# Splitting weight units ahead of their use, and storing transposed activations in pieces

## The chip, the cores and the metric

The kernel runs on one core of a Trainium2 chip. Its parts that matter here are TensorE (PE in the profile, with its weight loads as PEld), VectorE (DVE), ScalarE (ACT), GpSimd (POOL), and SyncE (SP), whose queue issues nearly all DMA transfers. The metric is the device time of one execution in microseconds, and the median of several runs is given.

## The reference, cut to what matters

An encoder layer is applied to two sequences of 1024 ("short") and 2048 ("long") tokens, each with 16 meta tokens in front; all weights are shared.

```python
xn = _rmsnorm(h, g_pre)
proj = xn @ w_in + b_in                      # 1024 -> 6672 columns
na_q, na_k, na_v, na_z, ml_qk, ml_v, ml_z, ml_o, ml_g, mg = split(proj)
ya = neighbourhood_attention(na_q, na_k, na_v, na_rpb)
ya = (ya * silu(na_z)) @ w_a
yb = (mlstm_branch(ml_qk, ml_v, ml_g, ml_o, ...) * silu(ml_z)) @ w_b
ga, gb = split(sigmoid(mg))                  # the gates: 2 x 1024 columns
y = (ga * ya + gb * yb) @ w_out              # the merge
return h + _rmsnorm(y, g_post)
```

All of it is in float32. The kernel makes each large product out of three products of a rounded high part and a low remainder: `hi*hi + hi*lo + lo*hi`. So every weight and every activation that enters a product is split first: ACT copies the high part, rounded to the type that PE takes, and DVE (for the first three units POOL) subtracts it from the original to get the low part.

## The kernel before, in words

The work is two streams of Python generators whose instructions are put into one program. The **dense** stream makes the projections and merges, the **sparse** stream the mLSTM and the neighbourhood attention. `run` takes steps of the two in turn by estimated costs; this fixes PE's order, which is written out by hand (`manual_schedule` for PE). The other engines' queues, SP's included, are ordered by the compiler's planner, which takes instructions in the order in which they become ready in its own model, the earlier written first.

The dense stream follows `PLAN`. A group `(s, t0, cols)` projects 1024 tokens of sequence `s` from token `t0` onto the columns of the mLSTM ("m"), the attention ("n") or the gates ("g"); `("f", s, b)` is a merge block of 512 tokens. The order is m and n of the short sequence, m of the long one's first half, m and n of its second half, g of the short sequence, its two merge blocks, and then the rest of the long sequence. The sparse stream follows `STEPS`: short mLSTM, short attention, long mLSTM, long attention.

*Weights.* A weight unit is 512 KB (some are 528): 128 columns of `w_in` by 1024 rows, or 256 columns by 512 rows, or the like of `w_a`, `w_b` and `w_out`. At its first use `wload` (L217) loads it into `wraw` (two buffers), `wpump` splits it (L235 on ACT, L238 on DVE) into `whi` and `wlo` (four buffers each) and stores both to DRAM (L242). At each later use `wpump` loads the stored halves back (L233). There are 68 units. 16 of them belong to the gates, 8 to `w_a` and `w_b`, 8 to `w_out`; these 32 are first used in the short sequence's gate group and its first merge block, beside the long mLSTM.

*Activations.* `build_half` normalises and transposes 512 tokens and splits them into `xh` and `xl` (two buffers each). Where a group of the same tokens comes much later in `PLAN`, it stores the two (L319), each with one transfer of 2 MB; the later group loads them back (L267). This is so for all six halves.

*A merge block* (`final`) multiplies the branch outputs, split by `yload` into `yh` and `yl` (L1217, L1218), with `w_a` and `w_b`, applies the gates `tg` (loaded at L1259, used at L1279 and L1281), splits the result into `mh` and `mlo` (L1282, L1283) and multiplies it with `w_out` (L1300 to L1302).

*The mLSTM* (`ml`) works on blocks of 256 tokens for four heads in turn: `raw`, `va` and `um` are its loads, `kf`, `num`, `den` and `hb` steps of its chain. `ml_norm` normalises 512 tokens of a head on DVE (`hb`, L1184 to L1197), and PE transposes them (L1202) at its place in the written order. The attention (`na`) prepares each head's `stk`, `kd` and `kx` on ACT and DVE (L638 to L645).

*Memory.* The sparse stream's pools lie on the right side of SBUF as a stack, the dense stream's long-lived pool `wp` on the left.

Of the kernel before, what the change touches and what calls it, by code (L numbers as in the profile page):

```python
# [9 lines left out]
F32 = mybir.dt.float32  # L10
F32R = mybir.dt.float32r
I32 = mybir.dt.int32
AF = mybir.ActivationFunctionType
ALU = mybir.AluOpType
# [3 lines left out]
P = 128  # L18
TCARGS = dict(schedule_with_timeline_sim=True)
D = 1024  # L20
KT = D // P
# [3 lines left out]
SEQLEN = (TP, TS)  # L25
# [5 lines left out]
C_MQ, C_MK, C_MV, C_MZ, C_MO, C_GA, C_GB = 2048, 2560, 3072, 3584, 4096, 4624, 5648  # L31
# [10 lines left out]
STEPS = (("ml", 0, ()), ("na", 0, (0, 1)), ("ml", 1, ()), ("na", 1, (0, 1, 2, 3)))  # L42
# [6 lines left out]
def _row_types(R):  # L49

    out = []
    for t in range(R // 8):
        if t == 0:
            out.append((0, 0, 11))
        elif t == R // 8 - 1:
            out.append((2, R - 12, 12))
        else:
            out.append((1, 8 * t - 4, 15))
    return out
# [51 lines left out]
class K:  # L111
# [3 lines left out]
    def __init__(self, tc, ins, outs):  # L115
        self.tc, self.nc = tc, tc.nc
        self.xs = []
        self.nu = 1
        self.i, self.o = ins, outs
        self.wreq, self.wraw, self.wrdy, self.wout = deque(), deque(), deque(), 0  # L120
        self.wseen, self.wkept, self.xkept = set(), {}, {}
        self.side = []


    def rsqrt8(self, pool, v, shape):
# [131 lines left out]
    def build_half(self, s, t0, meta, res, tags=("pj",), xp=None, per=4):  # L257

        nc, wp = self.nc, self.wp
        if (s, t0) in self.xkept:  # L260
            yield
            yield "scaled"
            x = []
            for name, part in zip(("xh", "xl"), self.xkept[s, t0]):
                x.append(wp.tile([P, KT, HALF], F32R, name=name, bufs=2))
                for k in range(0, KT, 4):
                    nc.sync.dma_start(x[-1][:, k:k + 4, :512].bitcast(F32), part[:, k:k + 4, :])  # L267
                yield
            res.append(tuple(x))
            return  # L270
        src = self.i["x_prompt" if s == 0 else "x_sample"]
        base = NM if meta else 0
        jobs = [(src[t0 + P * j:t0 + P * (j + 1), :], P, base + P * j) for j in range(4)]
        js = [jobs[a:a + per] for a in range(0, 4, per)]
        if meta:
            js[-1] = js[-1] + [(self.i["meta"], NM, 0)]
        xh = xl = None
        cnt = 0
        scaled = []
        for grp in js:  # L280
            xs = []
            for ap, n, col in grp:
                xr = (xp or wp).tile([P, D], F32, name="xr", bufs=5 if xp else 4)
                nc.sync.dma_start(xr[:n], ap)
                xs.append((xr, n, col))
            yield
            m = len(grp)
            ss = wp.tile([P, 5], F32, name="ss", bufs=2)
            nc.gpsimd.memset(ss, 1.0)
            for q, (xr, n, _) in enumerate(xs):  # L290
                junk = wp.tile([P, D], mybir.dt.bfloat16, name="xsq", tag="thT", bufs=1)
                nc.scalar.activation(junk[:n], xr[:n], AF.Square, accum_out=ss[:n, q:q + 1])
                yield
            nc.vector.tensor_scalar(ss[:, :m], ss[:, :m], 1.0 / D, EPS, op0=ALU.mult, op1=ALU.add)
            r = self.rsqrt8(wp, ss[:, :m], [P, m])
            yield
            for q, (xr, n, col) in enumerate(xs):
                nc.vector.scalar_tensor_tensor(xr[:n], xr[:n], r[:n, q:q + 1], self.gpre[:n], op0=ALU.mult, op1=ALU.mult)
                yield
            yield "scaled"  # L300
            if xh is None:
                xh = wp.tile([P, KT, HALF], F32R, name="xh", bufs=2)
                xl = wp.tile([P, KT, HALF], F32R, name="xl", bufs=2)
            for xr, n, col in xs:
                for e in range(2):
                    pt = self.psum(tags[cnt % len(tags)], [P, 4, P])
                    cnt += 1
                    for j in range(4):
                        nc.tensor.transpose(pt[:, j, :n], xr[:n, (4 * e + j) * P:(4 * e + j + 1) * P], self.ident[:n, :n])
                    h = xh[:, 4 * e:4 * e + 4, col:col + n]  # L310
                    nc.scalar.activation(h, pt[:, :, :n], AF.Copy)
                    nc.vector.tensor_tensor(xl[:, 4 * e:4 * e + 4, col:col + n], pt[:, :, :n], h.bitcast(F32), op=ALU.subtract)  # L312
                    yield
        where = [j for j, g in enumerate(PLAN) if g[:2] == (s, t0 // 1024 * 1024)]
        if where[-1] - where[0] >= len(where):
            self.xkept[s, t0] = []
            for x, part in ((xh, "h"), (xl, "l")):
                d = self.dp.tile([P, KT, 512], F32, name=f"x{part}{s}_{t0}")
                nc.sync.dma_start(d[:, :, :], x[:, :, base:base + 512].bitcast(F32))  # L319
                self.xkept[s, t0].append(d)  # L320
        res.append((xh, xl))


    def fm_evac(self, col, s, t0, meta, chunks, ps):
# [182 lines left out]
    def group(self, s, t0, meta, cols, reuse, nxt):  # L507

        todo = [(s, t0, meta), (s, t0 + 512, False)]
        jobs = self.layout(cols)  # L510
        nb = None
        for j, (kind, c) in enumerate(jobs):
            if kind == "tm":
                yield from self.tm_unit(c[0], [(x,) + h for x, h in zip(self.xs, todo)], c[1])
                continue
            ws = self.wtake(len(c))
            last = j == len(jobs) - 1
            for hf in range(2):
                side = None
                if j == 0 and hf == 0 and not reuse:  # L520
                    side = self.spread(self.build_half(*todo[1], self.xs), 15)
                elif last and nxt and nxt[0] == "f":
                    side = self.spread(self.ystart(*nxt[1:]), 15) if hf else None
                elif last and nxt:
                    if hf == 0:
                        nres = []
                        nb = self.build_half(*nxt, nres)
                        side = self.spread(nb, 15, "scaled")
                    else:
                        side = self.spread(nb, 15)  # L530
                for col, w in zip(c, ws):
                    for cost in self.fm_half(col, w, self.xs[hf], *todo[hf], done=self.wdone if hf else None):
                        yield cost
                        if side:
                            side()
                        if self.fout:
                            next(self.fout, None)
                if side:
                    side(True)
        if nb:  # L540
            self.xs = nres
# [870 lines left out]

    def sparse(self):

        for kind, s, rts in STEPS:
            if kind == "ml":
                for t0 in range(0, SEQLEN[s], 1024):
                    yield ("m", s, t0)
                yield from self.ml(s)
            else:  # L1420
                types = _row_types(SEQLEN[s] // 64)
                for t0 in range(0, SEQLEN[s], 1024):
                    if any((types[b][1] + types[b][2]) * 64 > t0 for b in rts):
                        yield ("n", s, t0)
                yield from self.na(s, rts)

    def run(self, ctx):
        self.done = set()
        self.setup(ctx)
        dense, acc = self.dense(ctx), 0.0  # L1430
        for w in self.sparse():
            if isinstance(w, tuple):
                while w not in self.done:
                    assert next(dense) is not True
                continue
            acc += w
            while acc > 0.0:
                d = next(dense, None)
                if d is None or d is True:
                    acc = 0.0  # L1440
                    break
                acc -= d
        for w in dense:
            assert w is not True
# [43 lines left out]
```

## Time and profile before

| what | value |
|---|---|
| median of 3 runs | 2904.53 us (2902.79 to 2905.13) |
| profiled execution, its own time | 2912.43 us |
| its span | 2910.7 us |
| PE, DVE, ACT busy | 2820.4, 1749.4, 1293.7 us |
| transferred | 661.88 MB, mean 227 GB/s |
| mean granted clock of PE | 0.989 |

Times in the profile are microseconds from the span's start. "A <- B" in a wait means that the engine of A stood idle until B released it. In a group, "busy, mean ns" are its total and the mean of one instruction; SPq rows are issues of transfers by SP. PEclk is the clock that PE was granted, as a share of full speed.

### The profile page before, as it was taken

How to read it: one execution, taken by the hardware profiler on the slowest of the kernel's cores; microseconds unless marked ns; L12 is line 12 of the kernel's file. 1: busy time of each engine (PE TensorE's matmuls, PEld its weight loads, DVE VectorE, ACT ScalarE, POOL GpSimd, SP SyncE). 2: the span in 40 equal slices, each digit the busy share in tenths (PEclk: the TensorE clock that was granted, in tenths of full speed). 3: DMA queues.
4: the chain of work that ended last, by engine and by line, in shares of the span. 5: the costliest groups of instructions: out<-in, count | busy, mean ns of one | idle time of the engine just before them, and what ended most of it. 6: DMA issues, size and time to landing. Idle time of an engine off the chain costs nothing.

```text
span 2910.7 us, 49314 instructions
## 1 busy us (share of the span) xinstructions
PE 2820.4 (97%) x17488; PEld 2513.6 (86%) x17488; DVE 1749.4 (60%) x4813; ACT 1293.7 (44%) x3114; POOL 23.4 (1%) x107
## 2 busy tenths in 40 slices
PE   6999999999999999999998999999999999999998
PEld 6998898899789988888886988898888888889887
DVE  5232576666556755467669778463555557777843
ACT  4112555444343444355655545453444445545421
POOL 1000000000000000000000000000000000000000
PEclk9999999999999999999999999999999999999999
DMA  9655576754775553578779798546659659888975
GB/s 349 221 178 180 198 230 235 269 185 161 246 233 171 186 170 123 173 249 273 233 249 316 265 341 293 176 140 196 200 180 293 207 166 262 259 289 253 304 255 193
DMA packets 436888, 661.88 MB, mean 227 GB/s; under 512 B 51136, under 2 KB 257296, under 8 KB 436640
## 3 DMA queue, kind: packets, MB, share of 16 engines
q1 hardware_dynamic: 435520, 656.03, 68.9%
q0 software_dynamic: 1120, 2.69, 0.4%
q8 instruction: 138, 2.26, 0.3%
q14 instruction: 110, 0.90, 0.1%
HBM read 447.97 MB, written 210.61 MB: 226 GB/s over the span
## 4 chain that ended last, share of the span: by engine, by line
PE 83%; DMA 9%; DVE 5%; ACT 1%; issue 1%; SPq 0%; DVEq 0%; ACTq 0%
PE pj L144 14%; PE pj L145 14%; PE pj L146 14%; PE pj L409 6%; PE pj L410 6%; PE pj L411 6%; PE sm L700 3%; PE pj L1302 3%; PE pj L1300 3%; PE pj L1301 3%; PE tr L688 3%; PE sc L663 1%; PE sc L664 1%; DMA tg<-gt 1%; PE sm L146 1%
## 5 line engine op out<-in xcount | busy, mean ns | idle before, releaser
L144 PE MATMUL pj<-xh,whi 128*128 128x512 f32 (+1 forms) x1824 | 717.1, 393 | 0.2 <-DVE xl L312 0.2
L145 PE MATMUL pj<-xl,whi 128*128 128x512 f32 (+1 forms) x1824 | 700.3, 384 | 0.4 <-DVE xl L312 0.4
L146 PE MATMUL pj<-xh,wlo 128*128 128x512 f32 (+1 forms) x1824 | 698.5, 383 | 0.0
L409 PE MATMUL pj<-whi,xh 128*128 128x256 f32 (+3 forms) x1576 | 451.8, 287 | 0.0
L410 PE MATMUL pj<-wlo,xh 128*128 128x256 f32 (+3 forms) x1576 | 445.7, 283 | 0.0
L411 PE MATMUL pj<-whi,xl 128*128 128x256 f32 (+3 forms) x1576 | 445.4, 283 | 0.0
L146 PEld LDWEIGHTS pj<-xh,wlo 128*128 128x128 f32 x1824 | 343.9, 189 | 72.1
L144 PEld LDWEIGHTS pj<-xh,whi 128*128 128x128 f32 x1824 | 344.3, 189 | 57.7 <-DVE xl L312 0.8
L145 PEld LDWEIGHTS pj<-xl,whi 128*128 128x128 f32 x1824 | 344.7, 189 | 55.6 <-DVE xl L312 0.7
L409 PEld LDWEIGHTS pj<-whi,xh 128*128 128x128 f32 (+1 forms) x1576 | 295.5, 188 | 1.5 <-issue 0.2
L410 PEld LDWEIGHTS pj<-wlo,xh 128*128 128x128 f32 (+1 forms) x1576 | 295.2, 187 | 1.1
L411 PEld LDWEIGHTS pj<-whi,xl 128*128 128x128 f32 (+1 forms) x1576 | 295.1, 187 | 0.9
L1300 PE MATMUL pj<-whi,mh 128*128 128x256 f32 x768 | 221.7, 289 | 0.0
L671 ACT ACTIVATE prb<-sc,mx 128x384 f32<-128x384 f32 (+2 forms) x192 | 120.1, 625 | 228.1 <-DVE mx L667 221.3
L1302 PE MATMUL pj<-whi,mlo 128*128 128x256 f32 x768 | 218.8, 285 | 1.9 <-DVE mlo L1283 1.9
L1301 PE MATMUL pj<-wlo,mh 128*128 128x256 f32 x768 | 218.4, 284 | 0.0
L691 DVE TENSOR_TENSOR pts<-tr,pts 96x512 fp32r<-96x512 f32 (+2 forms) x192 | 131.9, 687 | 119.2 <-ACT pts L690 117.5
L418 DVE TENSOR_TENSOR stT<-pj,bb 128x256 f32<-128x256 f32 (+3 forms) x197 | 83.3, 423 | 153.7 <-PE pj L411 150.4
L690 ACT ACTIVATE pts<-tr 96x512 fp32r<-96x512 f32 (+2 forms) x192 | 114.0, 594 | 115.9 <-PE tr L688 115.6
L667 DVE CUSTOM_DVE_ANT_1 sc<-sc,gt 128x384 f32<-128x384 f32 (+2 forms) x192 | 118.7, 618 | 76.1 <-PE sc L664 68.3
L144 PE MATMUL pj<-yh,whi 128*128 128x512 f32 x384 | 157.0, 409 | 7.4 <-DVE tg L1279 7.3
L706 DVE TENSOR_TENSOR yg<-sm,yg 64x128 f32<-64x128 f32 x384 | 108.3, 282 | 77.7 <-ACT yg L704 70.1
(233 smaller groups left out, 5123.7 us busy)
## 6 DMA issues: line engine op xcount, KB each, us to landing
whi<-wh SPq DMA_DIRECT2D x176, 512.0 KB
wlo<-wl SPq DMA_DIRECT2D x176, 512.0 KB
wh<-whi SPq DMA_DIRECT2D x64, 512.0 KB
wl<-wlo SPq DMA_DIRECT2D x64, 512.0 KB
wraw<-w_in SPq DMA_DIRECT2D x48, 512.0 KB
gt<-st SPq DMA_DIRECT2D x96, 256.0 KB
tg<-gt SPq DMA_DIRECT2D x96, 256.0 KB
xh<-xh SPq DMA_DIRECT2D x6, 2048.0 KB
```

Of the source, the lines that this page charges most:

```text
L144: mm(out, ah, bh, start=start, stop=False)
L145: mm(out, ah, bl, start=False, stop=False)
L146: mm(out, al, bh, start=False, stop=stop)
L409: nc.tensor.matmul(o, xh, wh, start=k == 0, stop=False)
L410: nc.tensor.matmul(o, xh, wl, start=False, stop=False)
L411: nc.tensor.matmul(o, xl, wh, start=False, stop=k == KT - 1)
L667: nc.vector.tensor_tensor_reduce(out=so, in0=so, in1=gt[:, g0:g0 + ns, c0:c0 + 32], op0=ALU.add, op1=ALU.min, scale=-1.0, scalar=3.0e38, a ...
L671: nc.scalar.activation(pr_[:, :N].rearrange("p (b a c) -> p b a c", b=4, c=8), sc[:, :N].rearrange("p (a b c) -> p b a c", b=4, c=8), AF.E ...
L691: nc.vector.tensor_tensor(pts[:ks, :, 1, :], pt[:ks], pts[:ks, :, 0, :].bitcast(F32), op=ALU.subtract)
L1300: nc.tensor.matmul(o, mh[:, k, xs], wh, start=k == 0, stop=False)
L1301: nc.tensor.matmul(o, mh[:, k, xs], wl, start=False, stop=False)
L1302: nc.tensor.matmul(o, ml[:, k, xs], wh, start=False, stop=k == KT - 1)
```

## The change

There are two parts. First, a generator `wprepare` goes through the 32 units of the gates, `w_a`, `w_b` and `w_out`: it loads a unit into a buffer of its own (`lw`), splits it (the high part into `hw`, the low part in place), and stores both halves to DRAM as `wpump` would have done. Its pool `wx` is opened ahead of the short mLSTM and closed behind it. In the dense stream `beside` is called behind every step of a group; from its 25th call on, every fourth call takes one of the three steps of a unit (load; split; store). What is left when the short mLSTM ends is done at once. When the gate group and the first merge block then ask for these units, `wpump` finds them stored and loads the halves.

Second, `build_half` no longer stores `xh` and `xl` itself but puts 16 pieces of 256 KB a half on a list, and every second call of `beside` issues one.

`sparse` is cut in two functions to hold the pool; the order of PE's work stays.

```diff
@@ __init__
-        self.side = []
+        self.xput, self.turn, self.wlater = deque(), 0, None
@@ build_half
             for x, part in ((xh, "h"), (xl, "l")):
                 d = self.dp.tile([P, KT, 512], F32, name=f"x{part}{s}_{t0}")
-                nc.sync.dma_start(d[:, :, :], x[:, :, base:base + 512].bitcast(F32))
+                self.xput.extend((d[:, k, :], x[:, k, base:base + 512].bitcast(F32)) for k in range(KT))
                 self.xkept[s, t0].append(d)
         res.append((xh, xl))
+
+    def beside(self):
+
+        self.turn += 1
+        if self.xput and self.turn % 2:
+            self.nc.sync.dma_start(*self.xput.popleft())
+        if self.wlater and self.turn > 24 and self.turn % 4 == 0:
+            next(self.wlater, None)
+
+    def wprepare(self, pool):
+
+        nc = self.nc
+        for key, srcs, nk, w in list(self.wreq):
+            if key in self.wseen or not (key[0] != "i" or key[1] >= C_GA):
+                continue
+            self.wseen.add(key)
+            lo = pool.tile([P, nk * w], F32, name="lw", bufs=1)
+            hi = pool.tile([P, nk * w], F32R, name="hw", bufs=1)
+            v = lo.rearrange("p (k c) -> p k c", k=nk)
+            k = 0
+            for s in srcs:
+                n = s.shape[0] // P
+                nc.sync.dma_start(v[:, k:k + n, :], s.rearrange("(k p) c -> p k c", p=P))
+                k += n
+            yield
+            nc.scalar.activation(hi, lo, AF.Copy)
+            nc.vector.tensor_tensor(lo.bitcast(F32R), lo, hi.bitcast(F32), op=ALU.subtract)
+            yield
+            self.wkept[key] = []
+            for x, part in ((hi, "h"), (lo, "l")):
+                d = self.dp.tile([P, nk * w], F32, name=f"w{part}{len(self.wkept)}")
+                nc.sync.dma_start(d[:, :], x.bitcast(F32))
+                self.wkept[key].append(d)
+            yield
@@ group
             if kind == "tm":
-                yield from self.tm_unit(c[0], [(x,) + h for x, h in zip(self.xs, todo)], c[1])
+                for cost in self.tm_unit(c[0], [(x,) + h for x, h in zip(self.xs, todo)], c[1]):
+                    yield cost
+                    self.beside()
                 continue
...
                         if self.fout:
                             next(self.fout, None)
+                        self.beside()
@@ sparse
+        with self.tc.tile_pool(name="wx", bufs=1, side="right", reuse_waits="tile") as wx:
+            yield from self.stage(*STEPS[0], wx)
+            for _ in self.wlater:
+                pass
+        self.wlater = None
+        for x in STEPS[1:]:
+            yield from self.stage(*x)
@@ run
             if isinstance(w, tuple):
-                while w not in self.done:
+                while w[:3] not in self.done:
                     assert next(dense) is not True
+                    if w[3:] and w[3] and not self.wlater:
+                        self.wlater = self.wprepare(w[3])
                 continue
```

`stage` holds the body of the old loop in `sparse`.

More of the change, by code (lines that the diff above doesn't have):

```diff
@@ L1413, in sparse, with stage @@
     def sparse(self):
[L1415 to L1425, printed above, removed]
+        with self.tc.tile_pool(name="wx", bufs=1, side="right", reuse_waits="tile") as wx:
[5 more added lines that the diff above has]
+            yield from self.stage(*x)
+    def stage(self, kind, s, rts, wx=None):
+        if kind == "ml":
+            for t0 in range(0, SEQLEN[s], 1024):
+                yield ("m", s, t0, wx)
+            yield from self.ml(s)
+        else:
+            types = _row_types(SEQLEN[s] // 64)
+            for t0 in range(0, SEQLEN[s], 1024):
+                if any((types[b][1] + types[b][2]) * 64 > t0 for b in rts):
+                    yield ("n", s, t0)
+            yield from self.na(s, rts)
     def run(self, ctx):
```

## The prediction

> **What bounds the kernel now.** I read the page first, then busy time by stretches, then the waits and timelines of the stretch that loses most.
>
> ```profile
> span 2910.7 us, 49314 instructions
> PE 2820.4 (97%) x17488; PEld 2513.6 (86%) x17488; DVE 1749.4 (60%) x4813; ACT 1293.7 (44%) x3114; POOL 23.4 (1%) x107
> ```
>
> TensorE (PE) works 97% of the span, in an order written by hand that the change leaves alone: no matmul is added, removed or moved. Only PE's idle time, 2910.7 - 2820.4 = 90.3 us, and time spent at a lowered clock can move. So I ask where the idle time lies.
>
> ```profile
> core 0: us, PE busy (x) PEld busy (x) DVE busy (x) ACT busy (x) POOL busy (x), PEclk, DMA share, GB/s
> 0.00:40.00 40.00, 16.95 (x97) 16.05 (x98) 28.83 (x61) 20.99 (x36) 8.37 (x22) 0.87 0.92 311
> 40.00:300.00 260.00, 259.61 (x1894) 243.17 (x1894) 70.13 (x145) 59.98 (x96) 0.46 (x9) 1.00 0.62 213
> 300.00:480.00 180.00, 176.83 (x1172) 158.90 (x1171) 110.27 (x317) 94.64 (x239) 3.23 (x19) 1.00 0.66 214
> 480.00:780.00 300.00, 297.17 (x2053) 273.62 (x2053) 191.58 (x605) 136.33 (x347) 3.43 (x15) 1.00 0.64 220
> ...
> 1270.00:1508.00 238.00, 238.00 (x1193) 198.74 (x1192) 155.01 (x457) 134.40 (x331) 0.71 (x5) 1.00 0.76 253
> 1508.00:1676.00 168.00, 151.02 (x922) 135.11 (x921) 144.55 (x423) 97.13 (x257) 0.29 (x3) 0.94 0.87 294
> 1676.00:1812.00 136.00, 132.90 (x860) 119.61 (x859) 107.08 (x351) 66.29 (x195) 0.40 (x3) 1.00 0.91 315
> ```
>
> By the code, 1270 to 1508 is the gate group of the short sequence (16 units split at first use), 1508 to 1676 the first merge block (the other 16), 1676 to 1812 the second merge block, which reloads its weights already split. All three run beside the long mLSTM. The gate group loses nothing. The first merge block loses 168.0 - 151.0 = 17.0 us, the second 3.1. The first merge block's waits:
>
> ```profile
> PE tr L1202 <- DVE hb L1197: 12.9, 1, 12.9
> PE sm L146 <- DVE ktl L966: 1.9, 1, 1.9
> PE pj L1302 <- DVE mlo L1283: 1.8, 1, 1.8
> ```
>
> Every one is for VectorE (DVE), which is 144.6/168 = 86% busy there against 79% in the second block. The DVE timeline up to the long wait, and the group of weight splits in this stretch (busy us, mean ns), show how much of it the change takes away:
>
> ```profile
> 1537.62 0.43 DVE L1056 TENSOR_TENSOR um<-um,trim 128x256 f32<-128x256 f32 x1 [2.01 <-DMA um<-ud]
> ...
> 1540.50 1.22 DVE L238 TENSOR_TENSOR wlo<-wraw,whi 128x1024 fp32r<-128x1024 f32 x1
> ...
> 1561.52 1.22 DVE L238 TENSOR_TENSOR wlo<-wraw,whi 128x1024 fp32r<-128x1024 f32 x1
> ...
> 1571.17 0.68 DVE L1197 TENSOR_TENSOR hb<-hb,szg 128x512 f32<-128x512 f32 x1
> ```
> ```profile
> L238 DVE TENSOR_TENSOR wlo<-wraw,whi 128x1024 fp32r<-128x1024 f32 x15 | 18.2, 1217 | 0.6 <-ACT whi L235 0.6
> ```
> ```profile
> L235 ACT ACTIVATE whi<-wraw 128x1024 fp32r<-128x1024 f32 x15 | 15.7, 1053 | 4.4 <-PE pj L145 2.2 <-DMA wraw<-w_out 2.2
> ```
>
> From 1537.6 to 1571.9 DVE has no gap, and four of the splits lie in that run (first and last are shown).
>
> **The change part by part.** *Splits leave the first merge block.* 15 ACT copies (15.7 us) and 15 DVE subtractions (18.2 us) go from this stretch; DVE falls to (144.6 - 18.2)/168 = 75%, under the second block's 79%. With equal work per matmul the second block is the nearest sample of what is left: 3.1/136 of idle, 3.8 us in 168. Gain 17.0 - 3.8 = 13.2 us. After the long wait PE also ran slowly:
>
> ```profile
> 1572.00 1.09 PE L1202 MATMUL tr<-ident,hb 128*128 128x128 f32 x4 [12.93 <-DVE hb L1197]
> 1572.74 0.78 PE L144 MATMUL pj<-yh,whi 128*128 128x512 f32 x1
> ...
> 1577.88 0.40 PE L144 MATMUL pj<-yh,whi 128*128 128x512 f32 x1
> 1578.11 0.39 PE L145 MATMUL pj<-yl,whi 128*128 128x512 f32 x1
> ```
>
> Twelve matmuls from 1572.74 to 1577.88 took 5.1 us where a spacing of 0.23 makes 2.8: 2.3 us more, which go with the wait. Together 15.5 us. PE is the bound from there to the end, so this shifts the end.
>
> *Transfers there.* Sizes of the weight and store issues:
>
> ```profile
> whi<-wh SPq DMA_DIRECT2D x176, 512.0 KB
> wh<-whi SPq DMA_DIRECT2D x64, 512.0 KB
> tg<-gt SPq DMA_DIRECT2D x96, 256.0 KB
> xh<-xh SPq DMA_DIRECT2D x6, 2048.0 KB
> ```
>
> A unit now costs 0.5 MB in and 1 MB out; after, two reloads of 0.5 MB. The gate and first merge stretches move 32 x 0.5 = 16 MB less. Reloads wait on SP's queue for PE to free their buffers, as the second block's do, at a DMA share of 0.91 with 3.1 us lost; I count nothing more. In the gate group, with no idle time, the cover is PE itself: nothing.
>
> *Splits arrive early.* 32 units x (0.5 + 1) MB = 48 MB move ahead, with 32 x 1.06 = 34 us of ACT and 32 x 1.22 = 39 us of DVE. By the code a step comes every fourth turn from turn 28; 32 x 3 steps end at turn 408, and the first two groups have 166 + 132 turns, so as traced the last lies in the third group, before the short mLSTM ends (its last store at 775). But only PE's order is by hand. The other queues take work as soon as the planner's buffers allow: in the timelines and the chain,
>
> ```profile
> 50.59 0.54 SPq L284 DMA_DIRECT2D xr<-x_sample  x1
> ```
> ```profile
> 775.05 0.41 SPq L1204 DMA_DIRECT2D yb<-hb  x1
> ```
> ```profile
> 308.19 4.24 DMA um<-ud
> 496.47 11.38 DMA um<-ud
> 762.99 14.47 DMA xl<-xl
> 777.53 9.05 DMA gain<-g_post
> 1541.74 4.83 DMA wl<-wlo
> 1589.58 5.15 DMA wraw<-w_out
> ```
>
> rows of the second sequence are loaded at 50.6, though the code asks for them in the last job of the second group, and the last gain vector at 777.5, though the code asks for it at the first merge block (1508). The split chain depends on nothing of PE's, so I expect it from the first 20 us on, paced only by its one buffer: 5.15 (load) + 1.06 + 1.22 + 4.83 (store) = 12.3 us a unit, 32 in 390 us, about 20 to 410. That adds 50.3 MB/390 us = 129 GB/s; at 0.62/213 of share per GB/s it is 0.38, on 0.62 to 0.66: a full DMA queue. What bounds the harm: PE loses 0.4 us in 40 to 300 and 3.2 in 300 to 480, DVE is 27% and 61% busy, and the chain has at most 1 MB under way, some 3 us of queue at 311 GB/s. An ordinary 4.24 us load becomes about 7. From below the cost is 0 (loads run ahead); from above see the third rival. I take 4 us, as much as these stretches lose now, mostly after 300, where the mLSTM's short chains feel a late load. The start adds little: its 23 us of idle end before there is much to split.
>
> *Stores of x in pieces.* Six halves, twice 2 MB, become 96 pieces of 256 KB. Now the um load at 496 takes 11.38 instead of 4.24, and near 763 a 2 MB store delays a gain load whose reader blocks DVE:
>
> ```profile
> 763.98 5.14 SPq L233 DMA_DIRECT2D whi<-wh  x1
> ```
> ```profile
> DVE gain L164 <- DMA gain<-g_post: 10.8, 1, 10.8
> ```
> ```profile
> PE sc L663 <- ACT kd L643: 2.0, 1, 2.0
> PE pj L309 <- DVE xl L312: 1.1, 1, 1.1
> PE pj L309 <- ACT st L345: 1.0, 1, 1.0
> ```
>
> Of PE's waits just behind this block (775 to 806), in the last fence, the stores bear on the 2.0 us on kd. The same bytes still go, and pieces too may run together, so from -2.0 to +2 us (84 more issues of some 0.5 us, of which SP has room); I take -1.
>
> Here the Trainium skill speaks against the change: "DMA: Bandwidth & Descriptors", section "Bandwidth", asks for transfers of 1 MiB or more, with a fixed 2.0 us per transfer by its fit. By that estimate eight pieces take 20.8 us where one store takes 6.8, and the 12 stores 168 us more of queue time. In rows, 315 GB/s ran in 1676 to 1812, where the merge block's gates come in pieces of 256 KB (tg), against 213 in 40 to 300. The trace does not bear the rule out for queued transfers.
>
> Sum against the profiled run: 2912.4 (span 2910.7 and 1.7 around it) - 15.5 + 4 - 1 = 2899.9. That run stands 7.9 above the median of 2904.5, so **2892.0** as a median.
>
> **The rivals.** *First: DVE's delay mostly stays.* Within the gapless run only four splits lie, each holding DVE 1.13 us: 4.5 us, and the gap at 1537.6 was a load's. If earlier splits are hidden anyway and the loads stay late, the gain is 4.5 and the net 4.5 - 4 + 1 = 1.5: 2903. Against it: nearly all DVE's idle time there is short, and stores of splits wait in SP ahead of those very loads.
>
> *Second: pieces cost queue time.* If each piece holds the queue for its own issue and landing, the stores near 490 and 763 stay in the way longer. Doubling the 2.0 + 1.1 + 1.0 = 4.1 us that PE idles from 775 to 806, in each of two such places, takes 8 and the 1 of the gain: 2901. The full rates above speak against it. By the skill's page and section named above it would be this way.
>
> *Third, slower: early splits block the engines.* ACT and DVE take their queues in order; a copy placed before its load has landed holds up all behind it, as the gain vector did for 10.8 us. PE idled 4.1 us behind that block. The place is 300 to 410, where mLSTM evacuations stand behind such a copy: 110/12.3 = 9 units, 9 x 4.1 = 37 us in place of the 4. Net +37 - 15.5 - 1 = +20.5: 2925. From four such blocks on (16.5 us) the gain is gone. For it: the DMA queue would be full, and plans are made ahead. Against: the units' loads are small, and a 1 MB backlog is 3 us, not 10.8.
>
> **How the numbers follow.** A measurement of this kernel tells 0.2% (5.8 us) from no change. Forecast 0.57, first rival 0.19, second 0.03, third 0.21. The forecast's own range is 2882 to 2900. The range of 8 in 10 reaches from 2878 (17.0, 2.3 and kd's 2.0 gone and no cost early make 2883; 5 more for another order of the queues) to 2918, which takes in the first two rivals and the milder half of the third. Faster: 0.55 of the forecast and 0.07 of the first two, 0.62. Same: the rest of those and the mildest of the third, 0.15. Slower: 0.23, most of the third and some of the first.
>
> **What would show it.** Right: no wlo split after 1000 us and 208 reloads of whi at 512 KB; in the first merge block DVE near 75% and no wait of over 5 us on hb; splits dense from 20 to about 410 us at a DMA share over 0.9, with PE idle there below 8 us. Wrong: the hb wait still 8 us or more (first rival); PE waits on ACT or DVE of several us each between 300 and 480, with ACT held by a raw load (third); later starts of loads behind the pieces near 490 and 763 (second).

## The result and the profile after

The change makes the kernel slower: 2933.9 us median (2928.0 to 2943.7) against 2904.8 of the kernel before on the same chip, ratio 1.0099 [1.0085, 1.0113], 29 us. The forecast was 12.5 us less, the third rival 20 us more.

The page of the kernel after (its profiled execution took 2935.3 us; from L358 on, lines of the kernel before stand 34 to 37 lines lower here):

```profile
span 2933.5 us, 49499 instructions
PE 2825.2 (96%) x17488; PEld 2516.4 (86%) x17488; DVE 1749.1 (60%) x4813; ACT 1294.8 (44%) x3114; POOL 22.8 (1%) x107
whi<-wh SPq DMA_DIRECT2D x206, 512.0 KB
wh<-hw SPq DMA_DIRECT2D x30, 512.0 KB
```

PE's busy time rose by 4.8 us, its idle time by 18. 30 units were split early (two had been loaded raw before the preparation reached them), so the change does what it says. Busy time by the same stretches, the later ones shifted by 20 us:

```profile
core 0: us, PE busy (x) PEld busy (x) DVE busy (x) ACT busy (x) POOL busy (x), PEclk, DMA share, GB/s
40.00:300.00 260.00, 256.29 (x1872) 240.92 (x1871) 85.15 (x150) 70.23 (x101) 0.46 (x9) 0.99 0.88 305
300.00:480.00 180.00, 167.72 (x1097) 150.45 (x1096) 114.91 (x321) 94.18 (x231) 2.71 (x19) 0.96 0.90 296
480.00:780.00 300.00, 291.91 (x2034) 270.58 (x2033) 192.46 (x601) 142.44 (x359) 3.36 (x15) 0.99 0.64 220
1528.00:1696.00 168.00, 153.54 (x936) 137.09 (x935) 131.26 (x409) 88.23 (x253) 0.29 (x3) 0.95 0.77 255
1696.00:1832.00 136.00, 134.89 (x870) 121.52 (x869) 109.15 (x356) 67.44 (x197) 0.40 (x3) 1.00 0.91 323
```

The three early stretches lose 3.7, 12.3 and 8.1 us of PE where they lost 0.4, 3.2 and 2.8. The first merge block lost 17.0 and still loses 14.5, at 78% of DVE and at a clock that is lowered as before. PE's waits in that block, and those from 285 to 520:

```profile
PE tr L1239 <- DVE den L1161: 8.4, 1, 8.4
PE pj L1339 <- DVE mlo L1320: 2.0, 2, 1.4
PE sc L145 <- DVE ql L1078: 1.5, 1, 1.5
PE sc L144 <- ACT qh L1077: 1.4, 1, 1.4
```
```profile
PE tr L999 <- DVE kf L963: 8.2, 1, 8.2
PE pj L309 <- DVE xl L312: 6.5, 2, 6.3
PE sm L810 <- ACT g_rg L807: 2.7, 1, 2.7
PE sm L146 <- DVE ktl L1003: 3.1, 3, 1.7
```

PE's 17488 matmuls come in the same order in all kernels here but late_norm. So each can be set against the same matmul of before's profiled run: "late at 520" is the start of the matmul that began at 520 there, minus that time. The kernel after is 0 late at 248, 5.3 at 302, 13.1 at 345, 19.4 at 447, 24.2 at 520, 27.9 at 842 and 25.9 at 1506. Most of the loss is made between 250 and 520, beside the short mLSTM. Behind 1506 the measure is poor: before's profiled run lies 7.9 above its median, and a kernel with the same work there (x_only) falls from 3.9 early at 1506 to 12.7 at the end.

### The profile page after: what moved, and what is told of

It reads as the page before. It is cut to its first block, busy times and chain, and to the rows that moved or that the text cites. A ratio compares the mean times of both kernels' runs of the same rounds, so it can differ in the third digit from the quotient of the medians.

```text
span 2933.5 us, 49499 instructions
## 1 busy us (share of the span) xinstructions
PE 2825.2 (96%) x17488; PEld 2516.4 (86%) x17488; DVE 1749.1 (60%) x4813; ACT 1294.8 (44%) x3114; POOL 22.8 (1%) x107
## 4 chain that ended last, share of the span: by engine, by line
PE 69%; DMA 11%; DVE 6%; issue 1%; ACT 1%; SPq 1%; DVEq 0%; ACTq 0%
PE pj L144 12%; PE pj L145 12%; PE pj L146 12%; PE pj L443 4%; PE pj L444 4%; PE pj L445 4%; PE pj L1339 3%; PE pj L1337 3%; PE pj L1338 3%; PE sm L737 3%; PE tr L725 3%; DMA tg<-gt 2%; DMA um<-ud 1%; PE sc L700 1%; PE sc L701 1%
## 5 line engine op out<-in xcount | busy, mean ns | idle before, releaser
L145 PE MATMUL pj<-yl,whi 128*128 128x512 f32 x384 | 152.7, 398 | 0.0
```

Source lines behind the costliest of these rows:

```text
L145: mm(out, ah, bl, start=False, stop=False)
```

## The experiments

Two theories at first. **A**: copies of the preparation that stand on ACT and DVE for a load hold up the mLSTM (the third rival). **B**: the preparation's traffic makes the mLSTM's own loads late. And for the late side: either it gains its 15 us and the early side costs 44, or it gains nothing.

### The parts by themselves

**x_only**: the diff of `build_half` and `beside` alone, `wlater` staying empty. **w_only**: the early splits, with x stored as before. **alias**: no early work, x as before; where a unit is first asked for, stored halves of another are loaded (so its values are not the layer's):

```
+        have = [k for k, d in self.wkept.items() if d[0].shape[1] == KT * P]
...
+            self.wkept[key] = self.wkept[have[n % len(have)]]
```

> Only the stores of x in 256 KB pieces; all weight units split at first use as before. Theory A (prepared splits block the in-order queues of ACT and DVE while their loads are on the way) and theory B (their 48 MB fill the DMA queue and the mLSTM's own loads land late) both say that the pieces cost little: 2905 plus or minus 4 us. Theory C (the pieces hold up the queue near 490 and 790) says 2912 or more.

> Only the early splits; x stored in 2 MB transfers as before. A and B: about 2930, nearly all of the change's +29. C: 2915 or less.

> No early work at all, x stored as before: the 32 units are neither loaded nor split nor stored; the gate group and the merge blocks load the stored halves of other units of the same size in their place (so the values are not the reference's). This is the late side of the change alone. If the prediction's term was right: 15.5 us gained, about 2889. If the gain is what the trace after shows between 1506 and 1695 (PE's lag falls by 4.7): about 2900.

x_only: 2902.6 us, ratio 0.9998 [0.9984, 1.0011]. w_only: 2922.8, 1.0067 [1.0047, 1.0087], 20.2 us late at 520. alias: 2906.4, 1.0010 [0.9999, 1.0021]. So the pieces alone cost nothing that can be seen, the late side gains nothing, and early splits account for two thirds of the loss. alias's stretch of the first merge block, its PE waits there, and DVE's waits for um between 1488 and 1600 in alias and (L1056, last row) before:

```profile
1508.00:1676.00 168.00, 154.73 (x928) 137.41 (x927) 129.56 (x410) 83.42 (x242) 0.50 (x4) 0.95 0.78 255
```
```profile
PE tr L1223 <- DVE hb L1218: 4.7, 2, 3.5
PE pj L1321 <- ACT mh L1303: 3.3, 1, 3.3
PE sc L144 <- ACT qh L1061: 2.1, 2, 1.7
PE sc L145 <- DVE ql L1062: 1.5, 1, 1.5
```
```profile
DVE um L1077 <- DMA um<-ud: 18.6, 9, 4.0
```
```profile
DVE um L1056 <- DMA um<-ud: 7.8, 6, 2.1
```

The hb wait falls from 12.9 to 4.7 us and DVE to 77%, nearly as forecast; but waits on mh, qh and ql come in its place, 13.3 us stay idle, and much of the time that DVE gained it stands waiting for loads of um.

### What holds the merge block

**late_norm**: the kernel before, with PE's transposes of hb six steps later (`for _ in range(14)` for `range(8)` in `ml_norm`). **um6** and **alias_um6**: six buffers for um in place of four, in the kernel before and in alias (room comes from keeping the added mask once and broadcasting it).

> The kernel before, with the transposes of the normalised mLSTM output written six steps later into PE's order (14 steps after the scaling instead of 8). On why taking all splits away gained nothing: if PE's 12.9 us wait on hb is set by the place of these transposes in PE's order against the length of the mLSTM's chain, the wait falls under 5 us and the time to about 2896. If it is DVE's load that makes it, the wait moves along and the time stays at 2904.

> The kernel before with the same six um buffers and nothing else. If um loads are no bound while DVE makes the late splits (DVE waits for um 7.8 us there), it stays within 0.15% of before (2900-2909); if they bind all mLSTM blocks, it falls by as much as alias_um6 does against alias.

> The late side alone (as in alias: the 32 units load stored halves of other units and no early work is done, so the values are not the reference's) and six um buffers in place of four; the mask that is added to um is kept once and broadcast over the two chunks to make room. In alias DVE waited 18.6 us in 9 waits for loads of um between 1488 and 1600, and the um loads are issued at the moment at which the buffer's last reader ends. If those loads hold the first merge block, its loads come 10 us earlier, the DVE waits for um in that stretch fall below 5 us and the time falls from alias's 2906 to 2890-2899. If the block is held by the rest of the long mLSTM's chain (scores, qh and ql, hb), the waits for um go but others take their place and the time stays at 2903-2909.

late_norm: 2913.1, 1.0027 [1.0016, 1.0038]. The wait on hb is gone, and in the stretch of the first merge block PE loses 8.8 us in place of 17.0, at a clock of 0.98 in place of 0.94:

```profile
1508.00:1676.00 168.00, 159.17 (x978) 141.88 (x977) 150.94 (x441) 99.39 (x267) 0.50 (x4) 0.98 0.94 320
```

So the place of these transposes in PE's order, and with it the hb wait, does set a part of what this block loses. But none of it is left at the end. By the count of matmuls PE is 18 us early at 2590 (x_only, with the work of before, 12.9) and level with before at 2872; from 2740 to 2860 it loses 10.4 us where before lost 4.4. The edit moves the transposes of every 512 tokens and so changes PE's order everywhere: it is no test of this block by itself.

um6: 2909.2, 1.0011 [1.0001, 1.0021]; alias_um6: 2909.1, 1.0015 [1.0005, 1.0025]. DVE's waits for um stay with six buffers (alias_um6):

```profile
DVE um L1076 <- DMA um<-ud: 18.1, 10, 4.0
```

So um's buffers are not what this block ends on. With the splits gone the hb wait shrinks and other waits of the mLSTM's chain take its place; which link of that chain sets its length isn't settled.

### Work and traffic apart

**split_only**: the kernel before plus 32 copies and subtractions of a resident tile, no transfers. **traffic**: the kernel before plus the early loads and two stores a unit of what was loaded, no early copy or subtraction, splits late as before. Both are pinned (below) at the change's pace. **pool_prep**: w_only with copy and subtraction on POOL. **ahead**: w_only in half units with three load buffers, each load two halves ahead of its copy.

```
pool_prep
+            nc.gpsimd.tensor_copy(hi, lo)
+            nc.gpsimd.tensor_tensor(lo.bitcast(F32R), lo, hi.bitcast(F32), op=ALU.subtract)
ahead
+                lo = pool.tile([P, n], F32, name="lw", bufs=3)
...
+            load(j + 2)
```

> As before, with 32 extra copies on ACT and subtractions on DVE of a resident tile at the places of the early splits, without any load or store (they produce nothing that is used). This is the engine time of the early splits by itself. A and B both say that the work is hidden: within 4 us of 2904. If the work itself were the cost: 2915 or more.

> The kernel before plus 30 to 32 early loads of 512 KB and 64 stores of 512 KB of what was loaded, pinned to the same places, with no early copy or subtraction and with the splits late as before: the traffic of the preparation without its work. If the price of paced is the work on ACT and DVE (split_only: about 9 us), this stays within 0.15% of before (2901-2909). If traffic holds up the short mLSTM's loads, it costs as much as or more than split_only: 2912-2920.

> As w_only, but the early copies and subtractions run on POOL, whose queue holds almost nothing else; loads and stores stay on SP's queue. ACT and DVE can't be blocked by them any more, though POOL's work may slow DVE while it runs. A: 2912 or less. B: 2920 or more, as w_only.

> As w_only, but the raw loads run ahead: units are handled in halves of 256 KB with three load buffers, so that each load is issued two halves before its copy. Bytes and work are the same, and the planner may run the chain faster. Theory A (queues of ACT and DVE blocked by copies that wait for their loads): the waits of ACT for prepared loads fall well under the 86 us of w_only, the time to 2912 or less. Theory B (the traffic itself delays the mLSTM's loads): no better than w_only, 2920 or more.

split_only: 2914.7, 1.0028 [1.0018, 1.0038]. traffic: 2910.7, 1.0021 [1.0010, 1.0031]. pool_prep: 2926.9, 1.0066 [1.0050, 1.0083]. ahead: 2927.3, 1.0067 [1.0049, 1.0084]. Work alone or traffic alone costs 6 to 9 us, and neither reaches w_only's 19. Both theories had put the work alone at nothing. ahead is no clean test of A: up to 600 us its copies stand 51.5 us for stores that must free their buffers, besides the loads.

pool_prep looked as if it refuted A, but it brings a price of its own. DVE groups from 300 to 480, before and in pool_prep (busy us, mean ns):

```profile
L853 DVE SCALAR_TENSOR_TENSOR cv<-raw,cw,cv 128x256 f32<-128x256 f32 (+1 forms) x34 | 15.3, 451 | 4.9 <-ACT cv L850 4.4
L418 DVE TENSOR_TENSOR stT<-pj,bb 128x256 f32<-128x256 f32 (+1 forms) x18 | 7.5, 415 | 3.7 <-PE pj L411 3.6
```
```profile
L890 DVE SCALAR_TENSOR_TENSOR cv<-raw,cw,cv 128x256 f32<-128x256 f32 (+1 forms) x34 | 20.5, 602 | 5.9 <-ACT cv L887 5.6
L1093 DVE TENSOR_TENSOR um<-um,trim 128x256 f32<-128x256 f32 x14 | 9.6, 710 | 18.7 <-DMA um<-ud 18.7
L452 DVE TENSOR_TENSOR stT<-pj,bb 128x256 f32<-128x256 f32 (+1 forms) x18 | 7.4, 411 | 0.0
```

DVE operations with two SBUF operands took 602 in place of 451 ns on average in this stretch with POOL's work (um plus its mask 710; 424 in w_paced), while one with an operand in PSUM kept 411. The Trainium skill, "SBUF — State Buffer", section "Who interferes with whom", says the same: a DVE instruction with two SBUF inputs contends with a GpSimd instruction that reads SBUF. The rows agree. The 12 late weight splits in that stretch kept 1219 ns, but none of them ran while POOL was at work; six others in the same run overlapped one of POOL's subtractions and took 1599 to 3157 ns.

### The planner's placing

**paced**: the whole change, with the preparation's loads, copies, subtractions and stores pinned to the place at which they are written (`keep_in_program_order`). **w_paced**: the same with x as before. **pin_dma**: w_only with the preparation's loads and stores alone pinned.

```
paced, w_paced (pin_dma: the two dma_start lines alone)
-                nc.sync.dma_start(v[:, k:k + n, :], s.rearrange("(k p) c -> p k c", p=P))
+                pin(nc.sync.dma_start(v[:, k:k + n, :], s.rearrange("(k p) c -> p k c", p=P)))
...
+            pin(nc.scalar.activation(hi, lo, AF.Copy))
...
+                pin(nc.sync.dma_start(d[:, :], x.bitcast(F32)))
```

> The whole change, with each load, copy, subtraction and store of the early splits held behind everything written earlier for its engine, so that the planner can't pull it ahead of its place. Same bytes, same work. A: ACT's waits for the prepared loads fall from 92 us to under 25, PE's lag at 780 from 28 to under 12 us, time about 2910. B: the traffic is the same and only a little later, so the time stays at 2925 or more.

> As paced (early splits with their loads, copies, subtractions and stores pinned to their places), with x stored in 2 MB pieces as before. If the pieces cost nothing beside a pinned preparation, it equals paced (2911-2918). If the pieces bring the load that shifts the short mLSTM, it falls to split_only's price, 2906-2911 plus a few us of traffic. If the pieces help, it is over 2918.

> w_only with the preparation's loads and stores alone pinned, and its copies and subtractions placed by the planner. Theory C: the transfers set how many units lie between 285 and 520, so it equals w_paced: 2911-2918. If the copies' and subtractions' placing on ACT and DVE costs, it stays at w_only's 2918-2926.

paced: 2914.2, 1.0033 [1.0022, 1.0044]. w_paced: 2913.8, 1.0025 [1.0014, 1.0036]. pin_dma: 2913.7, 1.0034 [1.0020, 1.0047]. Pinning the transfers alone takes away half of w_only's price, and with pinned transfers the pieces cost nothing. The same work and the same bytes are done, so this half of the price lies in when the transfers are issued.

### The pace

Between 285 and 520 the pinned units lie about 21 us apart, the planner's 16. **Theory C**: between 285 and 520 the transfers are full with 11 units, and each more costs 5 us. **Theory D**: the number doesn't matter, the planner's order does. **dense**: w_paced with a step at every third place. **dense_x**: that with x in pieces. **gap**: dense, ending after 16 units (the last copy at 307 us). **spread**: the 16 units of gap with a step at every sixth place. **traffic_dense**: traffic at the pace of dense.

```
-        if self.wlater and self.turn > 24 and self.turn % 4 == 0:
+        if self.wlater and self.turn > 24 and self.turn % 3 == 0:      (spread: % 6)
```

> As w_paced (pinned, x in 2 MB pieces), with a step of the preparation at every third place in place of every fourth: about 15 units in place of 11 between 285 and 520. Theory C (the stretch is full with 11): 51.8 MB and 15 times 1.5 MB are 74 MB, at 290 GB/s 256 us in place of 235, so PE is 15 to 25 us late at 520 and the time is 2924-2934. Theory D (what costs is the planner's placing): pinned units stay cheap, PE is under 8 us late at 520 and the time stays at 2911-2918.

> As dense, with x in 256 KB pieces. Theory C: the pieces add no bytes, so 2924-2936 as dense, a few us more if the pieces shift more units into the stretch. If the pieces have a price of their own beside a dense preparation (after against w_only, 11 us), it is 8-12 us over dense. Theory D: 2911-2920.

> As dense, but the preparation ends after 16 units, so that nearly all lie before 285 and none between 300 and 520; the other units are split late as in the kernel before. Theory C: nothing is late at 520 (under 2 us) and the time is within 0.1% of before, 2902-2908. If the work or the traffic costs wherever it lies, half of w_paced's price stays: 2909-2911 or more.

> The 16 units of gap, with a step at every sixth place in place of every third: about 32 us apart from 90 to 580, some 7 of them between 285 and 520; the same work and bytes as gap. If the pace costs (theory C): 51.8 MB and 7 times 1.5 MB are 62 MB, under the 68 MB that the stretch takes in; PE is under 4 us late at 520 and the time is 2904-2911. If 16 units cost what they cost wherever they lie, it equals gap: 2916-2922.

> As traffic (the preparation's loads, and stores of what was loaded, with no early copy or subtraction and the splits late as before), at the pace of dense: a step at every third place. Theory C, transfers alone: the same 74 MB between 285 and 520 as dense, so PE is 15 to 23 us late at 520 and the time is 2920-2930. If the copies and subtractions in ACT's and DVE's queues are what makes dense late, PE is under 5 us late at 520 and the time stays near traffic's 2911. Late by 5 to 15: each has a part.

dense: 2929.8, 1.0089 [1.0069, 1.0109]. dense_x: 2940.1, 1.0120 [1.0101, 1.0139]. gap: 2919.2, 1.0053 [1.0035, 1.0070]. spread: 2910.1, 1.0012 [1.0001, 1.0023]. traffic_dense: 2922.9, 1.0055 [1.0039, 1.0071].

Theory D falls with dense: pinned, and as dear as the planner's order. C names the time of dense and spread rightly but falls with gap, which has two units in the stretch and is 8.0 us late at 520. Bytes don't order the kernels either. What moved (packets, bytes, rate) from 285 to 520 in w_paced (2.9 us late), after (24.2) and gap (8.0):

```profile
DMA packets 57617, 67.18 MB, mean 286 GB/s; under 512 B 4400, under 2 KB 44888, under 8 KB 57595
```
```profile
DMA packets 57435, 68.02 MB, mean 289 GB/s; under 512 B 4466, under 2 KB 45683, under 8 KB 57415
```
```profile
DMA packets 47937, 55.75 MB, mean 237 GB/s; under 512 B 3924, under 2 KB 36969, under 8 KB 47916
```

What goes with the lateness is how long SP's queue stood at the preparation's own transfers in that stretch (sum over the waits of its load and store lines):

| kernel | units in it | SP stood, us | late at 520, us | ratio |
|---|---|---|---|---|
| spread | 7 | 3.1 | 2.8 | 1.0012 |
| pin_dma | 11 | 9.6 | 6.9 | 1.0034 |
| w_paced | 11 | 10.8 | 2.9 | 1.0025 |
| paced | 11 | 10.8 | 3.0 | 1.0033 |
| traffic | 11 | 11.0 | 0.6 | 1.0021 |
| gap | 2 | 14.3 | 8.0 | 1.0053 |
| ahead | 13.5 | 24.7 | 10.7 | 1.0067 |
| traffic_dense | 15 | 25.2 | 13.7 | 1.0055 |
| dense_x | 15 | 36.4 | 20.9 | 1.0120 |
| dense | 14 | 39.9 | 22.4 | 1.0089 |
| after | 15 | 42.6 | 24.2 | 1.0099 |
| w_only | 15 | 44.4 | 20.2 | 1.0067 |
| pool_prep | 12 | 11.5 | 17.4 | 1.0066 |

From gap down, 43 to 57% of SP's standing returns as PE's lateness; above it, the 0.6 to 6.9 us of lateness are near the 4.0 that split_only has with no transfers at all. pool_prep, with its slowed DVE, is the exception.

This is a correlation and no more. SP stands for the kernel's own transfers too, and in all it stood less in this stretch in after (116 us) than in before (141). ACT's waits for the preparation's loads go along with the lateness as well (4.1 us in spread, 11.1 in w_paced, 21.4 in dense, 22.2 in after, 29.6 in w_only); but they don't tell gap (7.1) from w_paced, and traffic_dense has none. The ratios also hold up to 14 us more than the lateness at 520 (dense_x); by the traces most kernels lose another 2 to 7 us between 520 and 842, and where the rest lies is open.

Three places in the timelines show how a unit holds PE up. The first is ahead of the short mLSTM's loads; the kernel before, then after:

```profile
289.36 0.27 ACT L770 ACTIVATE g_rg<-sm 1x36 f32<-1x36 f32 x2 [1.24 <-PE sm L768]
```
```profile
293.45 1.06 ACT L347 ACTIVATE hw<-lw 128x1024 fp32r<-128x1024 f32 x1 [4.41 <-issue]
294.41 0.25 ACT L807 ACTIVATE g_rg<-sm 1x36 f32<-1x36 f32 x2
294.63 0.30 PE L810 MATMUL sm<-ident,g_cm 36*1 36x36 f32 x2 [2.72 <-ACT g_rg L807]
```

A unit's copy stands 4.4 us in ACT's queue ahead of the mLSTM's g_rg. The profile names no releaser here; in dense and gap such a copy holds g_cm in the same way, and there the 4.4 and 4.6 us are put down to the unit's load. PE waits 2.7 us, runs at a lowered clock behind it (0.80 on average from 290 to 298), and is 5.3 us late at 302. This is theory A and the third rival.

The second place is the mLSTM's first loads; before, then after:

```profile
300.27 0.35 SPq L358 DMA_DIRECT2D nq<-st  x1
300.67 0.42 SPq L841 DMA_DIRECT2D raw<-mk  x1
304.55 0.51 ACT L850 ACTIVATE cv<-raw,cw 128x256 f32<-128x256 f32 x1 [4.30 <-DMA raw<-mk]
```
```profile
299.00 0.39 SPq L344 DMA_DIRECT2D lw<-w_in  x1
303.21 1.06 ACT L347 ACTIVATE hw<-lw 128x1024 fp32r<-128x1024 f32 x1 [1.26 <-DMA lw<-w_in]
304.29 0.35 SPq L353 DMA_DIRECT2D wh<-hw  x1
305.57 0.34 SPq L392 DMA_DIRECT2D nq<-st  x1
306.01 0.39 SPq L353 DMA_DIRECT2D wl<-lw  x1
306.45 0.44 SPq L878 DMA_DIRECT2D raw<-mk  x1
311.18 0.51 ACT L887 ACTIVATE cv<-raw,cw 128x256 f32<-128x256 f32 x1 [5.63 <-DMA raw<-mk]
317.44 0.43 DVE L1093 TENSOR_TENSOR um<-um,trim 128x256 f32<-128x256 f32 x1 [3.01 <-DMA um<-ud]
```

SP issues the unit's load at 299.0 and then stands at its first store until the copy has ended (304.27). Yet this standing is not what makes the raw load late. In both kernels the raw load goes out behind a store of st (nq), which waits for a product of PE, and PE is 5.3 us late already; only the unit's second store, 0.4 us, comes between them. The raw load is used 6.6 us later than before. Ahead of kf, DVE then stands 3.0 us for a load of um and makes a late split, and PE waits 8.2 us for kf.

In the third place, after again, SP's queue does hold a load of the mLSTM:

```profile
491.77 0.38 SPq L344 DMA_DIRECT2D lw<-w_out  x1
492.25 0.97 SPq L1052 DMA_DIRECT2D um<-ud  x2
495.72 1.06 ACT L347 ACTIVATE hw<-lw 128x1024 fp32r<-128x1024 f32 x1 [4.00 <-DMA lw<-w_out]
496.70 0.42 DVE L1093 TENSOR_TENSOR um<-um,trim 128x256 f32<-128x256 f32 x1 [4.26 <-DMA um<-ud]
501.07 1.11 PE L309 MATMUL pj<-ident,xr 128*128 128x128 f32 x4 [6.31 <-DVE xl L312]
```

SP stood 2.6 us at the unit's load, whose buffer was still being stored, so the um loads behind it went out 1.2 us after sl, the last reader of their buffers, had ended (491.04). The first is used 4.5 us after its issue (492.25), against 3.2 in before. DVE stands 4.3 us for it, ACT 4.0 us at the unit's copy, which stands ahead of the next xh; the unit's subtraction (1.2 us) comes ahead of xl too, and PE waits 6.3 us.

So three things come together: SP's queue standing at a unit, a copy ahead of its load in ACT's queue, and loads that arrive later. No run put the preparation's transfers on another queue or took SP's standing away alone, so their shares aren't shown. traffic_dense, with no early copy, keeps 16 of dense's 26 us by the ratios and 13.7 of its 22.4 us of lateness. So at that pace the transfers by themselves are the larger part; that the work on ACT and DVE makes the rest is inferred.

None of the kernels beats the one before.

## Why the prediction was wrong

- **Splits leave the first merge block (15.5 us): the term that failed on the gain's side.** Measured +0.10% [-0.01, 0.21] in alias. DVE fell nearly as forecast, but "the second block is the nearest sample of what is left" did not hold: 13.3 us stay idle against 3.8, with other waits of the mLSTM's chain in place of hb's, and the slow clock stayed (0.95 against 0.94). That a shorter block "shifts the end" isn't borne out either: late_norm's 8 us didn't reach the end, though it changes more than this block.
- **The first rival** (DVE's delay mostly stays, gain 4.5) is the nearest to what the late side did. Its gapless run with four splits was the better reading, but the gain was nothing, not 4.5.
- **Splits arrive early (4 us): the step that decides the sign.** Fullness was right (a DMA share of 0.88 to 0.90), and the place nearly: units from 32 to 548 us where 20 to 410 were named, since a unit took 16 us or more and not 12.3. The mis-sized term is its price, 18.7 us in w_only. The step priced a slower transfer ("4.24 becomes 7") and bounded the harm by PE's former losses. It did not price what a unit does in queues that are taken in order: its copy ahead of its load on ACT, its stores and its buffer on SP.
- **Pieces of x (-1 us):** by themselves not told from nothing, 0.9998 [0.9984, 1.0011], nor beside pinned splits; the second rival's 9 us did not come. Beside dense splits they cost 10 us (dense_x against dense; after against w_only 11). Where these lie is open: dense_x is no later than dense at 520. The 168 us more of queue time that the prediction worked out for the pieces left no mark on x_only's time. The Trainium skill's "DMA: Bandwidth & Descriptors", section "Bandwidth", gives its table, and the page its fit with the fixed 2.0 us, for transfers issued from GpSimd. These are stores issued by SP, so the run doesn't speak for or against it.
- **The third rival** had the sign, and its marks came (PE waits of several us between 300 and 480, ACT held by a raw load). Its mechanism is seen where the loss starts: g_rg behind a unit's copy, 5.3 us. That its 20 us come near the measured 29 is in part luck, for they count in the 15.5 us of gain that never came. And it isn't the whole: ACT waited for the preparation's loads for 22.2 us between 285 and 520 (19.1 of it on loads of w_out), but with no early copies at all (traffic_dense) 13.7 us of lateness remain.
- The step put no price on the early copies and subtractions themselves; split_only shows 0.28% for them, beside a PE that is 98% busy.

## What to carry to other kernels

Work that is moved off a visible wait gains only what the next wait leaves: change the late side alone before paying for the early one. Price a moved step by every in-order queue that it stands in: a copy whose load is still under way, and a store or load that must wait for a copy or a buffer; ask what stands behind each. Where such steps fall matters more than their number: gap's 16 units cost 0.53%, and all its 8 us of lateness come at the last two of them, at the start of the short mLSTM; the 16 units of spread, twice as far apart, cost 0.12%.

## What the runs showed of the hardware

- 96 stores of 256 KB cost no more than 12 of 2 MB when queued beside products (x_only).
- POOL subtractions on 128x1024 took 2481 ns against DVE's 1220. DVE operations on two SBUF operands that overlapped one took up to 2617 ns (um plus its mask, median 424) and 3157 (a weight split).
- From 285 to 520, where such loads and stores are mixed, no kernel moved more than 302 GB/s (dense_x); dense and traffic_dense moved 299.
